# A PEER block's second down pass splits its stored activations again, with 9 of 32 blocks kept on chip

## The chip, the cores and the metric

The kernel runs on one core of one Trainium2 chip. A core has TensorE (matrix products; PE in the profile, and PEld for its weight loads), VectorE (DVE), ScalarE (ACT), GpSimd (POOL) and SyncE (SP), each with an instruction queue of its own that is executed in order. Data comes from HBM and goes back to it over 16 DMA engines. Here SP issues nearly all loads, POOL issues the indirect gathers and some stores, and ACT issues a few stores. The metric is the device time of one execution in microseconds.

## The reference, cut to what matters

```python
# D_MODEL 2048, 256 tokens, 8 PEER heads, 128 x 128 experts, 16 experts taken per head
mod = silu(c) @ w_ada + b_ada                     # 96 columns of 128 values: "ada"
h = rms_norm(x, g_norm1) * (1 + sc1) + sh1
x = x + gt1 * token_mixer(h, ...)                 # sparse attention, pooling, gates
h = rms_norm(x, g_norm2) * (1 + sc2) + sh2
# PEER: experts and gates from two product-key top-16 lists per head, then per token
a   = gelu(h . peer_u[experts])                   # up
out = sum_e (a * gate)[e] * peer_v[experts[e]]    # down
x = x + gt2 * out
```

All data is float32.

## The kernel before

**Token mixing.** The first part of the program does the ada sums, the input projection, the attention, the pooling branch and the output projection. Its order is made by a scheduler. Float32 weights arrive in tiles `raw` of 1 MB (128 x 2048), of which there are four in a ring (`RAW`). Each half of a tile is split into a rounded high part `wH` (ACT, line 124) and a rest `wL` (DVE, line 125), and TensorE multiplies the parts. An "ada" is one of the 96 columns of `mod`: a 1 MB load into the same ring, then a DVE multiply-and-sum over 128 x 2048 (line 139). 64 of them are not needed at once. They stand in a list `bg`, and the loops of the token mixing take from it at given rates: `R_Y` per round in the two loops of 16 rounds over `ybr` (the pooling branch, line 509, and the attention branch, line 532), `R_GA`, `R_WO` and `R_PQ` in others. The 16 last are GT2, needed only by the final step.

**PEER, done densely for 224 tokens.** From here on the order is written by hand: every engine runs its instructions in the order of the code. The *up* stage goes over all 128 x 128 experts, 128 at a time, in 256 halves `k`; a half is 16 matmuls against 1024 of the 2048 features, from a half tile of `u`. The activations of 128 experts go through Gelu and are stored to DRAM (`adram`). The gates are built as a dense table in DRAM (`gdram`) meanwhile. The *down* stage goes twice over 128 groups of 128 experts (`e`), 8 output blocks in each pass: pass 1 (`hf` 0) for features 0 to 1023, pass 2 (`hf` 1) for the rest. A group is again 16 matmuls, 8 of them 448 columns wide (high weights with both parts of the activations) and 8 of 224 (low weights with the high part). Weights are half tiles of `v`; one load brings two groups.

In pass 1 the activations of four groups are a block `h`, 32 blocks in all. For each block SP loads `ab` from `adram` (448 KB), for each two blocks a gate table `gb` from `gdram` (896 KB, one buffer); DVE multiplies (`gate_mul`, line 905), ACT and DVE split the product into the pair `aHL` (lines 910, 911), POOL stores the pair to `sdram` (896 KB, line 915), and in pass 2 SP loads it again (`gate_reload`, line 919; two buffers, freed by TensorE). Loads of `v` are issued three tiles ahead of use.

**PEER for the other 32 tokens** is done sparsely, beside all this: 32 gathers of 1 MB from the rows of `u` (one expert row for each of 128 token-and-slot partitions), each followed by a DVE multiply-and-sum (line 814), then 32 gathers from the rows of `v`, each followed by a DVE multiply-add (line 833). Two gather buffers: `fetch(n + 2)` is issued by POOL after the sum over buffer `n`. These, the routing, the gates and the leftover adas are one long generator of side work. After each half or group the code calls `spend(rate)`, which adds `rate` microseconds of DVE time to a credit and runs side work until it is used up:

```python
R_UP, R_D1, R_D2 = 0.85, 0.55, 0.9
def spend(budget):
    credit[0] = min(credit[0] + budget, 4.0)
    while credit[0] > 0.0:
        cost = next(work, "end")
        if cost is None or cost == "end":
            return cost
        credit[0] -= cost
```

So these rates set how fast gathers are asked for in the up stage, in pass 1 and in pass 2.

Of the kernel before, what the change touches and what calls it, by code (L numbers as in the profile page):

```python
# [9 lines left out]
F32 = mybir.dt.float32  # L10
F32R = mybir.dt.float32r
# [3 lines left out]
ALU = mybir.AluOpType  # L15
# [4 lines left out]
P = 128  # L20
T = 256
D = 2048
ND = 16
# [6 lines left out]
N = T - AS  # L30
# [1 line left out]
KGROUPS = ((0, 4), (4, 10), (10, 16))  # L32
NGU = 43
RAW = 4
R_K, R_Y, R_GA, R_WO, R_PQ = 0.6, 0.4, 0.7, 0.6, 0.3
TB = 8
R_UP, R_D1, R_D2 = 0.85, 0.55, 0.9
GATE_SCALE = 2.0 ** 15


# [1 line left out]
def kernel(  # L42
# [23 lines left out]
    nc = tc.nc  # L66
    wgrp_in = (wgrp0_in, wgrp1_in, wgrp2_in)
    dve, act, pe = nc.vector, nc.scalar, nc.tensor

    const = ctx.enter_context(tc.tile_pool(name="const", bufs=1))  # L70
    main = ctx.enter_context(tc.tile_pool(name="main", bufs=1))
    stream = ctx.enter_context(tc.tile_pool(name="stream", bufs=3))
    dram = ctx.enter_context(tc.tile_pool(name="dram", bufs=1, space=DRAM))
# [3 lines left out]
    hHL = main.tile([P, ND, 2, T], F32R, name="hHL")  # L77
# [211 lines left out]
    while ada_next[0]:  # L289
        f, i = ada_next[0].pop(0)  # L290
        f(i)
    for gi, (ka, kb) in enumerate(KGROUPS):
# [5 lines left out]
        for r in range(ntiles):  # L298
            us = list(range(per * r, min(per * r + per, NGU)))
            n = len(us) * nb * P  # L300
# [202 lines left out]
    for j in range(ND):  # L503
# [3 lines left out]
        for k in range(8):  # L507
            o = 1024 * (j % 2) + P * k
# [114 lines left out]
    px = ctx.enter_context(tc.tile_pool(name="px", bufs=1))  # L623
# [106 lines left out]

    gdram = dram.tile([P, N // 16, P, 16], F32, name="gdram")
    adram = dram.tile([P, P, N], F32, name="adram")
    sdram = dram.tile([P, P // 4, 4, 2, N], F32, name="sdram")
    made = {}

    def gates_build(x):
# [154 lines left out]
    def half(k):  # L891
        return split(raws[k // 2][:, 1024 * (k % 2):1024 * (k % 2) + 1024])

    def gate_load(h):
        made["ab", h] = px.tile([P, 4, N], F32, name="ab", bufs=3)
        nc.sync.dma_start(out=made["ab", h], in_=adram[:, 4 * h:4 * h + 4])

    def gate_table(b):
        made["gb", b] = px.tile([P, N // 16, 8, 16], F32, name="gb")
        nc.sync.dma_start(out=made["gb", b], in_=gdram[:, :, 8 * b:8 * b + 8])  # L900

    def gate_mul(h):
        i = 4 * (h % 2)
        av = made["ab", h].rearrange("p i (g t) -> p i g t", t=16)
        dve.tensor_tensor(av, av, made["gb", h // 2][:, :, i:i + 4].rearrange("p g i t -> p i g t"), ALU.mult)

    def gate_split(h):
        src = made["ab", h]
        aHL = px.tile([P, 4, 2, N], F32R, name="aHL", bufs=2)
        act.copy(aHL[:, :, 0], src)  # L910
        dve.tensor_tensor(aHL[:, :, 1], src, aHL[:, :, 0], ALU.subtract)
        made["act", h] = aHL

    def gate_store(h):
        nc.gpsimd.dma_start(out=sdram[:, h], in_=made["act", h].bitcast(F32))

    def gate_reload(h):
        aHL = px.tile([P, 4, 2, N], F32R, name="aHL", bufs=2)
        nc.sync.dma_start(out=aHL.bitcast(F32), in_=sdram[:, h])
        made["act", P // 4 + h] = aHL  # L920

    def mm2(ps, w, off, xHL, start, stop):
        wH, wL = w[0][:, off:off + P], w[1][:, off:off + P]
        pe.matmul(ps[:, :2 * N].rearrange("p (a n) -> p a n", a=2), wH, xHL, start=start, stop=False)  # L924
        pe.matmul(ps[:, :N], wL, xHL[:, 0], start=False, stop=stop)  # L925
# [9 lines left out]
    def ahead(k):  # L935
        if k % 2 == 0:
            fetch_tables(k // 2 + 3)
        if k + 2 < 4 * P:
            ws[k + 2] = half(k + 2)
        due = pend[:]  # L940
        del pend[:]
        for f in due:
            f()

    def up_add(e, ps):
        if e % 4 == 0:
# [12 lines left out]
    for k in range(2 * P):  # L959
        e, f = k // 2, k % 2  # L960
        ahead(k)
        if f == 0:
            ps = accp.tile([P, 512], F32, name="acc")
        w = ws.pop(k)
        for d in range(8):
            mm2(ps, w, d * P, hHL[:, 8 * f + d, :, AS:], f == 0 and d == 0, f == 1 and d == 7)
        if f == 1:
            pend.append(lambda e=e, ps=ps: up_add(e, ps))
        spend(R_UP)
        if k == 2 * P - 24:  # L970
            assert made["gates"] == T // TB - 1
            gate_table(0)
            for h in range(3):
                gate_load(h)
        if k in (2 * P - 8, 2 * P - 7):
            gate_mul(k - 2 * P + 8)
        if k == 2 * P - 6:
            gate_table(1)
        if k == 2 * P - 5:
            gate_split(0)  # L980
        if k == 2 * P - 4:
            gate_load(3)
            gate_store(0)

    def flush(j, ps, last):
        x, gt = xT[:, j, AS:], mod[:, GT2 + j:GT2 + j + 1]
# [21 lines left out]
    for hf in range(2):  # L1008
        assert hf == 0 or made["gt2"]
        po = [accp.tile([P, 512], F32, name="acc") if q < 6 else gps.tile([P, 512], F32, name="gp") for q in range(8)]  # L1010

        def products(e, w, j):
            mm2(po[j], w, P * j, made["act", 32 * hf + e // 4][:, e % 4], e == 0, e == P - 1)

        for e in range(P):
            k = 2 * P + P * hf + e
            h = e // 4
            if e < P - 1:
                ahead(k)
            if e < P - 2:  # L1020
                w = ws.pop(k)
                for j in range(8):
                    products(e, w, j)
            elif e == P - 1:
                w = [ws.pop(k - 1), ws.pop(k)]
                for j in range(8):
                    for i in range(2):
                        products(P - 2 + i, w[i], j)
                    flush(8 * hf + j, po[j], hf)
                ahead(k)  # L1030
            if hf == 0:
                b = e // 8
                if e % 8 in (3, 4) and b + 1 < P // 8:
                    gate_mul(2 * b + e % 8 - 1)
                if e % 8 == 5 and b + 2 < P // 8:
                    gate_table(b + 2)
                if e % 4 == 1 and h + 1 < P // 4:
                    gate_split(h + 1)
                if e % 4 == 2 and h + 1 < P // 4:
                    gate_store(h + 1)  # L1040
                    if h + 4 < P // 4:
                        gate_load(h + 4)
                if e == P - 2:
                    gate_reload(0)
            elif e % 4 == 1 and h + 1 < P // 4:
                gate_reload(h + 1)
            done = spend(R_D2 if hf else R_D1)
            if hf and done == "end" and "sum" not in made:
                made["sum"] = True
                pend.append(lambda: sparse_sum(po))  # L1050
                pend.append(lambda: pend.append(lambda: sparse_out(po)))
# [80 lines left out]
```

## Time and profile before

| | |
|---|---|
| median of 3 runs | 2226.87 us (2224.63 to 2232.24) |
| profiled execution | 2226.57 us, of which the span of the profile is 2224.8 us |
| busy share of the span | PE 94%, PEld 89%, DVE 75%, ACT 45%, POOL 6% |
| DMA | 677.91 MB, mean 305 GB/s |
| mean granted clock of TensorE | 0.968 of full speed |

Matmuls overlap in their pipeline, so the busy share of PE is not a share of its peak. What a stage loses is read from how many matmuls it completes in a stretch of time, and from who waits for whom there.

### The profile page before, as it was taken

How to read it: one execution, taken by the hardware profiler on the slowest of the kernel's cores; microseconds unless marked ns; L12 is line 12 of the kernel's file. 1: busy time of each engine (PE TensorE's matmuls, PEld its weight loads, DVE VectorE, ACT ScalarE, POOL GpSimd, SP SyncE). 2: the span in 40 equal slices, each digit the busy share in tenths (PEclk: the TensorE clock that was granted, in tenths of full speed). 3: DMA queues.
4: the chain of work that ended last, by engine and by line, in shares of the span. 5: the costliest groups of instructions: out<-in, count | busy, mean ns of one | idle time of the engine just before them, and what ended most of it. 6: DMA issues, size and time to landing. Idle time of an engine off the chain costs nothing.

```text
span 2224.8 us, 35362 instructions
## 1 busy us (share of the span) xinstructions
PE 2100.6 (94%) x14192; PEld 1981.4 (89%) x14192; DVE 1675.9 (75%) x2392; ACT 1011.9 (45%) x1373; POOL 136.5 (6%) x129
## 2 busy tenths in 40 slices
PE   6999999999989999999999999888899989999999
PEld 4899987999989999999999999777888888889998
DVE  7898877769787787778887776666777667777755
ACT  3543442754444455555555555343444334333334
POOL 0000000000000000000000000011112111222200
PEclk7999999999999999999999999988999999999999
DMA  8888875678775566776667778899999999999985
GB/s 340 328 318 309 309 264 217 227 294 311 288 280 193 186 225 234 252 258 238 235 225 256 259 281 294 337 332 373 403 392 400 397 378 389 415 412 415 415 309 199
DMA packets 146997, 677.91 MB, mean 305 GB/s; under 512 B 11737, under 2 KB 42481, under 8 KB 98321
## 3 DMA queue, kind: packets, MB, share of 16 engines
q1 hardware_dynamic: 125986, 549.63, 67.6%
q0 software_dynamic: 16240, 111.36, 12.4%
q10 hardware_dynamic: 4608, 14.68, 1.7%
q8 instruction: 111, 1.82, 0.3%
q14 instruction: 52, 0.43, 0.0%
HBM read 614.76 MB, written 60.83 MB: 304 GB/s over the span
## 4 chain that ended last, share of the span: by engine, by line
PE 57%; DMA 17%; issue 16%; DVE 7%; ACT 2%; POOL 0%; SPq 0%; ACTq 0%; DVEq 0%; POOLq 0%
PE acc L924 18%; PE acc L925 9%; PE acc L136 7%; PE acc L134 7%; PE acc L135 7%; DMA raw<-in_v_dram 6%; DMA raw<-in_ada_dram 6%; DMA aHL<-sdram 4%; PE gp L924 3%; DVE wL L125 3%; PE acc L509 2%; DVE raw L139 2%; PE gp L925 1%; ACT wH L124 1%; DMA raw<-in_wgrp_dram 1%
## 5 line engine op out<-in xcount | busy, mean ns | idle before, releaser
L124 ACT CAST wH<-raw 128x1024 fp32r<-128x1024 f32 (+2 forms) x738 | 750.8, 1022 | 1032.5 <-PE gp L924 311.4
L125 DVE TENSOR_TENSOR wL<-raw,wH 128x1024 fp32r<-128x1024 f32 (+2 forms) x738 | 871.3, 1188 | 387.5 <-ACT wH L124 385.2
L924 PE MATMUL acc<-hHL,wH 128*128 128x448 f32 x2048 | 653.4, 376 | 0.5 <-ACT r L600 0.5
L924 PE MATMUL acc<-aHL,wH 128*128 128x448 f32 x1536 | 526.2, 390 | 31.0 <-DMA aHL<-sdram 15.3
L925 PE MATMUL acc<-hHL,wL 128*128 128x224 f32 x2048 | 545.0, 266 | 10.9 <-DVE wL L125 10.8
L925 PE MATMUL acc<-aHL,wL 128*128 128x224 f32 x1536 | 421.8, 275 | 38.0 <-DVE wL L125 38.0
L924 PEld LDWEIGHTS acc<-hHL,wH 128*128 128x128 f32 x2048 | 385.3, 188 | 29.5 <-ACT r L600 0.7
L925 PEld LDWEIGHTS acc<-hHL,wL 128*128 128x128 f32 x2048 | 391.7, 191 | 12.3 <-DVE wL L125 12.3
L134 PE MATMUL acc<-hHL,wH 128*128 128x256 f32 x1200 | 344.9, 288 | 18.4 <-ACT wH L124 17.3
L924 PEld LDWEIGHTS acc<-aHL,wH 128*128 128x128 f32 x1536 | 302.5, 197 | 60.0 <-ACT wH L124 16.9
L925 PEld LDWEIGHTS acc<-aHL,wL 128*128 128x128 f32 x1536 | 307.8, 200 | 44.8 <-DVE wL L125 44.7
L136 PE MATMUL acc<-hHL,wL 128*128 128x256 f32 x1200 | 340.7, 286 | 5.3 <-DVE wL L125 5.2
L135 PE MATMUL acc<-hHL,wH 128*128 128x256 f32 x1200 | 341.6, 285 | 0.1
L139 DVE CUSTOM_DVE_ANT_0 raw<-raw,cb 128x2048 f32<-128x2048 f32 x96 | 219.6, 2287 | 67.2 <-DMA raw<-in_ada_dram 67.1
L134 PEld LDWEIGHTS acc<-hHL,wH 128*128 128x128 f32 x1200 | 232.0, 194 | 22.9 <-ACT wH L124 20.6
L136 PEld LDWEIGHTS acc<-hHL,wL 128*128 128x128 f32 x1200 | 231.2, 193 | 7.4 <-DVE wL L125 7.2
L135 PEld LDWEIGHTS acc<-hHL,wH 128*128 128x128 f32 x1200 | 232.4, 194 | 0.7 <-DVE hHL L573 0.3
L924 PE MATMUL gp<-aHL,wH 128*128 128x448 f32 x512 | 182.5, 386 | 0.0
L925 PE MATMUL gp<-aHL,wL 128*128 128x224 f32 x512 | 138.1, 270 | 0.0
L924 PEld LDWEIGHTS gp<-aHL,wH 128*128 128x128 f32 x512 | 100.1, 196 | 8.2
L925 PEld LDWEIGHTS gp<-aHL,wL 128*128 128x128 f32 x512 | 101.6, 198 | 0.0
L833 DVE SCALAR_TENSOR_TENSOR hs<-r,wS,hs 128x2048 f32<-128x2048 f32 x31 | 72.8, 2349 | 7.8 <-DMA r<-in_v_dram,idxS 7.8
(247 smaller groups left out, 1978.9 us busy)
## 6 DMA issues: line engine op xcount, KB each, us to landing
raw<-in_u_dram SPq DMA_DIRECT2D x128, 1024.0 KB, 5.1
raw<-in_v_dram SPq DMA_DIRECT2D x128, 1024.0 KB, 13.5
raw<-in_ada_dram SPq DMA_DIRECT2D x96, 1024.0 KB, 5.5
raw<-in_wgrp_dram SPq DMA_DIRECT2D x43, 768.0 KB, 6.1
sdram<-aHL POOLq DMA_DIRECT2D x32, 896.0 KB, 10.5
aHL<-sdram SPq DMA_DIRECT2D x32, 896.0 KB, 9.6
raw<-in_ybr_dram SPq DMA_DIRECT2D x16, 1024.0 KB, 5.4
raw<-in_wga_dram SPq DMA_DIRECT2D x16, 1024.0 KB, 4.8
```

Source lines behind the costliest of these rows:

```text
L124: act.copy(wH[:, :n], src)
L125: dve.tensor_tensor(wL[:, :n], src, wH[:, :n], ALU.subtract)
L134: pe.matmul(ps, wH, xH, start=start, stop=False, **kw)
L135: pe.matmul(ps, wH, xL, start=False, stop=False, **kw)
L136: pe.matmul(ps, wL, xH, start=False, stop=stop, **kw)
L139: dve.tensor_tensor_reduce(raw, raw, cb, scale=1.0, scalar=0.0, op0=ALU.mult, op1=ALU.add, accum_out=modr[:, i:i + 1])
L509: pe.matmul(ps, ybr[0][:, o:o + P], pooled[k], start=k == 0, stop=k == 7)
L833: dve.scalar_tensor_tensor(made["o"], rows, wS[:, n:n + 1], made["o"], op0=ALU.mult, op1=ALU.add)
L924: pe.matmul(ps[:, :2 * N].rearrange("p (a n) -> p a n", a=2), wH, xHL, start=start, stop=False)
L925: pe.matmul(ps[:, :N], wL, xHL[:, 0], start=False, stop=stop)
```

## The change

Pass 2 no longer loads split pairs. The gated product is written back as one float32 block (448 KB) over its place in `adram`, loaded again in pass 2 and split there again by ACT and DVE, so `gate_load` and `gate_split` now run over 64 block numbers. Nine of the 32 blocks (`h` = 3, 6, ... 27) are not stored at all: their product is written into the 32 KB per partition of `hHL`, which the up stage has finished with, and both passes split it from there. The rates change too: more adas in the two `ybr` loops (`R_Y`), more side work per half in the up stage (`R_UP`), less per group in the down passes.

```diff
-R_K, R_Y, R_GA, R_WO, R_PQ = 0.6, 0.4, 0.7, 0.6, 0.3
+R_K, R_Y, R_GA, R_WO, R_PQ = 0.6, 0.75, 0.7, 0.6, 0.3
-R_UP, R_D1, R_D2 = 0.85, 0.55, 0.9
+R_UP, R_D1, R_D2 = 0.97, 0.3, 0.75
+KEPT = 9
...
+    def kept(h):
+        return h % 3 == 0 and 0 < h <= 3 * KEPT
+
+    def gate_load(n):
+        h = n % (P // 4)
+        if n >= P // 4 and kept(h):
+            return
+        made["ab", n] = px.tile([P, 4, N], F32, name="ab", bufs=3)
+        nc.sync.dma_start(out=made["ab", n], in_=adram[:, 4 * h:4 * h + 4])
...
     def gate_mul(h):
+        if kept(h):
+            if "keep" not in made:
+                made["keep"] = main.tile([P, ND, 2, T], F32R, name="hHL").rearrange("p a b t -> p (a b t)")
+            o = 4 * N * (h // 3 - 1)
+            dst = made["keep"][:, o:o + 4 * N].bitcast(F32).rearrange("p (i n) -> p i n", n=N)
+            made["ab", P // 4 + h] = dst
+        else:
+            dst = made["ab", h]
...
+        made["ab", h] = dst
+        if not kept(h):
+            nc.gpsimd.dma_start(out=adram[:, 4 * h:4 * h + 4], in_=dst)
+
+    def gate_split(n):
+        src = made["ab", n]
...
-    def gate_store(h):
-        nc.gpsimd.dma_start(out=sdram[:, h], in_=made["act", h].bitcast(F32))
-
-    def gate_reload(h):
-        aHL = px.tile([P, 4, 2, N], F32R, name="aHL", bufs=2)
-        nc.sync.dma_start(out=aHL.bitcast(F32), in_=sdram[:, h])
-        made["act", P // 4 + h] = aHL
...
-                if e % 4 == 2 and h + 1 < P // 4:
-                    gate_store(h + 1)
-                    if h + 4 < P // 4:
-                        gate_load(h + 4)
-                if e == P - 2:
-                    gate_reload(0)
-            elif e % 4 == 1 and h + 1 < P // 4:
-                gate_reload(h + 1)
+            b, n = e // 8, 32 * hf + h
...
+            if e % 4 == 1 and n + 1 < 2 * (P // 4):
+                gate_split(n + 1)
+            if e % 4 == 2 and n + 4 < 2 * (P // 4):
+                gate_load(n + 4)
```

The change moves instructions on three queues. On POOL, at the end of the up stage and the start of pass 1, before (the `r_...` rows are gathers, `sdram<-aHL` the stores of pairs):

```order
L783 DMA gdram<-hs 128x2048 x14
L809 DMA r_14718<-in_urow_dram,idxS 128x2048 x7
L915 DMA sdram<-aHL 128x1792
L809 DMA r_14718<-in_urow_dram,idxS 128x2048
L915 DMA sdram<-aHL 128x1792
```

and at the same place in the changed program (its lines are numbered one higher):

```order
L783 DMA gdram<-hs 128x2048 x14
L809 DMA r_14327<-in_urow_dram,idxS 128x2048 x18
L923 DMA adram<-ab 128x896
L809 DMA r_14327<-in_urow_dram,idxS 128x2048
L923 DMA adram<-ab 128x896
```

18 gathers instead of 7 now stand ahead of the first store, and a store has half the bytes. Counted by the split of a weight half behind which they stand, before there are 6 `u` sums at halves 229 to 255 (with 6 adas among them), then 23 in pass 1 (with 6 adas) and 3 at the start of pass 2, and all 32 `v` sums in pass 2. In the changed program there are 19 `u` sums at halves 211 to 256 (with 2 adas), 13 `u` and 3 `v` sums in pass 1, and 29 `v` sums in pass 2, the last at its group 91 of 128.

On SP, in pass 2, before (`raw<-in_v_dram` are the weights, `aHL<-sdram` the pairs):

```order
L919 DMA aHL<-sdram 128x1792
L887 DMA raw<-in_v_dram 128x2x1024 x2
L919 DMA aHL<-sdram 128x1792
L887 DMA raw<-in_v_dram 128x2x1024 x2
L919 DMA aHL<-sdram 128x1792
```

and there in the changed program:

```order
L902 DMA ab<-adram 128x896
L887 DMA raw<-in_v_dram 128x2x1024 x2
L902 DMA ab<-adram 128x896
L887 DMA raw<-in_v_dram 128x2x1024 x4
L902 DMA ab<-adram 128x896
```

A pair of 896 KB for every two weight loads has become a block of 448 KB, and where a kept block falls there is no load. On DVE, in the middle of the attention branch of the token mixing, before (`ISA raw,modr` is an ada sum, `sg` and `m_...` the merging of the branches, `wL` a weight split):

```order
L139 ISA modr 128x1
L532 TENSOR_TENSOR sg<-acc,m_4880 128x256
L125 TENSOR_TENSOR wL<-raw,wH 128x1024
L533 TENSOR_TENSOR sg<-sg,r_253 128x256
L532 TENSOR_TENSOR sg<-acc,m_4944 128x256
L125 TENSOR_TENSOR wL<-raw,wH 128x1024
L536 TENSOR_TENSOR m_5684<-sg,pl 128x256
L533 TENSOR_TENSOR sg<-sg,r_253 128x256
L532 TENSOR_TENSOR sg<-acc,m_5005 128x256
L139 ISA raw,modr<-raw,cb 128x2048
```

and in the changed program:

```order
L533 TENSOR_TENSOR sg<-acc,m_4748 128x256
L140 ISA raw,modr<-raw,cb 128x2048
L140 ISA modr 128x1
L534 TENSOR_TENSOR sg<-sg,r_253 128x256
L533 TENSOR_TENSOR sg<-acc,m_4827 128x256
L140 ISA raw,modr<-raw,cb 128x2048
L140 ISA modr 128x1
L537 TENSOR_TENSOR m_5633<-sg,pl 128x256
L534 TENSOR_TENSOR sg<-sg,r_253 128x256
L533 TENSOR_TENSOR sg<-acc,m_4898 128x256
```

Between the first and the last row of line 532 (533 in the changed program) there are now 10 ada sums instead of 5 and 13 weight splits instead of 15. In the pooling branch (first to last row of line 510) there are 10 adas instead of 7, and the one ada that stood between the last output projection and the second normalisation is gone.

## Rows read from the trace of the kernel before

**Rows 1.** Windows by stage: start:end, length, each engine's busy time, PEclk, DMA share, GB/s.
```profile
318.00:405.00 87.00, 85.71 (x408) 66.43 (x408) 62.58 (x156) 23.83 (x61) 0.00 (x0) 0.98 0.53 197
511.00:560.00 49.00, 49.00 (x411) 49.00 (x410) 48.29 (x77) 23.13 (x33) 0.00 (x0) 1.00 0.89 320
...
768.00:1380.00 612.00, 611.31 (x4171) 578.59 (x4172) 480.71 (x796) 334.88 (x455) 16.82 (x26) 1.00 0.71 247
1380.00:1458.00 78.00, 67.57 (x411) 63.54 (x410) 53.38 (x56) 32.67 (x42) 7.29 (x6) 0.93 0.91 336
1458.00:1868.00 410.00, 355.76 (x2052) 329.80 (x2050) 288.68 (x267) 160.87 (x166) 56.19 (x56) 0.91 1.01 386
1868.00:2118.00 250.00, 237.72 (x1454) 224.37 (x1455) 187.52 (x136) 97.54 (x95) 53.02 (x32) 0.97 1.01 410
```
**Rows 2.** Timeline of DVE, end of pass 2: start, length, idle before and its releaser.
```profile
2135.03 1.23 DVE L125 TENSOR_TENSOR wL<-raw,wH 128x1024 fp32r<-128x1024 f32 x1 [1.28 <-ACT wH L124]
...
2212.74 1.22 DVE L125 TENSOR_TENSOR wL<-raw,wH 128x1024 fp32r<-128x1024 f32 x1 [1.28 <-ACT wH L124]
```
**Rows 3.** Timeline of TensorE's weight loads, between the two passes.
```profile
1868.47 0.29 PEld L924 LDWEIGHTS acc<-aHL,wH 128*128 128x128 f32 x1 [3.90 <-DVE xT L990]
```
**Rows 4.** Waits in pass 1: waiting engine, releaser, us in total, times, longest.
```profile
ACT wH L124 <- DMA raw<-in_v_dram: 128.7, 31, 9.5
...
PEld acc L925 <- DVE wL L125: 44.7, 23, 11.0
...
DVE raw L139 <- DMA raw<-in_ada_dram: 29.7, 6, 10.5
```
**Rows 5.** DMA in pass 1: the sum, then issues by tensor with KB each, us to landing.
```profile
DMA packets 56807, 158.10 MB, mean 386 GB/s; under 512 B 2777, under 2 KB 27904, under 8 KB 52924
...
raw<-in_v_dram SPq DMA_DIRECT2D x65, 1024.0 KB, 14.5
sdram<-aHL POOLq DMA_DIRECT2D x31, 896.0 KB, 10.3
ab<-adram SPq DMA_DIRECT2D x28, 448.0 KB, 12.2
gb<-gdram SPq DMA_DIRECT2D x14, 896.0 KB, 10.4
...
r<-in_urow_dram,idxS POOLq DMA_INDIRECT x25, 9.8
```
**Rows 6.** The same for pass 2 up to its last gather.
```profile
DMA packets 20181, 102.53 MB, mean 410 GB/s; under 512 B 1607, under 2 KB 1607, under 8 KB 15941
...
aHL<-sdram SPq DMA_DIRECT2D x22, 896.0 KB, 10.1
r<-in_v_dram,idxS POOLq DMA_INDIRECT x32, 10.0
```
**Rows 7.** Instructions by line, whole run: count | busy us, mean ns | idle before.
```profile
L139 DVE CUSTOM_DVE_ANT_0 raw<-raw,cb 128x2048 f32<-128x2048 f32 x96 | 219.6, 2287 | 67.2 <-DMA raw<-in_ada_dram 67.1
...
L814 DVE CUSTOM_DVE_ANT_0 r<-r,hs 128x2048 f32<-128x2048 f32 x32 | 73.1, 2285 | 0.0
...
L809 POOL DMA_INDIRECT r<-in_urow_dram,idxS x32 | 50.2, 1568 | 330.9 <-DVE aS L814 330.3 <-issue 0.6
...
L911 DVE TENSOR_TENSOR aHL<-ab,aHL 128x896 fp32r<-128x896 f32 x32 | 34.7, 1085 | 0.0
...
L910 ACT CAST aHL<-ab 128x896 fp32r<-128x896 f32 x32 | 30.0, 936 | 0.0
```
**Rows 8.** The chain that ended last, before the second normalisation.
```profile
656.07 2.20 DVE raw L139
```
**Rows 9.** Waits at the end of the up stage (1380 to 1458 us).
```profile
DVE raw L139 <- DMA raw<-in_ada_dram: 11.5, 2, 11.2
PEld acc L925 <- DVE wL L125: 11.3, 3, 9.8
```
**Rows 10.** Waits of SP's DMA queue in pass 1.
```profile
SPq L900 <- DVE ab L905: 121.6, 13, 14.1
```

More of the change, by code (lines that the diff above doesn't have):

```diff
@@ L732 @@
     adram = dram.tile([P, P, N], F32, name="adram")
-    sdram = dram.tile([P, P // 4, 4, 2, N], F32, name="sdram")
     made = {}
@@ L892, in half @@
         return split(raws[k // 2][:, 1024 * (k % 2):1024 * (k % 2) + 1024])
-    def gate_load(h):
-        made["ab", h] = px.tile([P, 4, N], F32, name="ab", bufs=3)
-        nc.sync.dma_start(out=made["ab", h], in_=adram[:, 4 * h:4 * h + 4])
+    def kept(h):
[6 more added lines that the diff above has]
+        nc.sync.dma_start(out=made["ab", n], in_=adram[:, 4 * h:4 * h + 4])
     def gate_table(b):
@@ L902, in gate_mul @@
     def gate_mul(h):
-        i = 4 * (h % 2)
[L904 to L908, printed above, removed]
+        if kept(h):
[6 more added lines that the diff above has]
+            dst = made["ab", h]
+        i = 4 * (h % 2)
+        dve.tensor_tensor(dst.rearrange("p i (g t) -> p i g t", t=16),
+                          made["ab", h].rearrange("p i (g t) -> p i g t", t=16),
+                          made["gb", h // 2][:, :, i:i + 4].rearrange("p g i t -> p i g t"), ALU.mult)
+        made["ab", h] = dst
[3 more added lines that the diff above has]
+        src = made["ab", n]
         aHL = px.tile([P, 4, 2, N], F32R, name="aHL", bufs=2)
@@ L911, in gate_split @@
         dve.tensor_tensor(aHL[:, :, 1], src, aHL[:, :, 0], ALU.subtract)
-        made["act", h] = aHL
-    def gate_store(h):
-        nc.gpsimd.dma_start(out=sdram[:, h], in_=made["act", h].bitcast(F32))
-    def gate_reload(h):
-        aHL = px.tile([P, 4, 2, N], F32R, name="aHL", bufs=2)
-        nc.sync.dma_start(out=aHL.bitcast(F32), in_=sdram[:, h])
-        made["act", P // 4 + h] = aHL
+        made["act", n] = aHL
     def mm2(ps, w, off, xHL, start, stop):
@@ L982 @@
             gate_load(3)
-            gate_store(0)
     def flush(j, ps, last):
@@ L1030 @@
                 ahead(k)
[L1031 to L1038, printed above, removed]
-                if e % 4 == 2 and h + 1 < P // 4:
-                    gate_store(h + 1)
-                    if h + 4 < P // 4:
-                        gate_load(h + 4)
-                if e == P - 2:
-                    gate_reload(0)
-            elif e % 4 == 1 and h + 1 < P // 4:
-                gate_reload(h + 1)
+            b, n = e // 8, 32 * hf + h
+            if hf == 0 and e % 8 in (3, 4) and b + 1 < P // 8:
+                gate_mul(2 * b + e % 8 - 1)
+            if hf == 0 and e % 8 == 5 and b + 2 < P // 8:
+                gate_table(b + 2)
+            if e % 4 == 1 and n + 1 < 2 * (P // 4):
+                gate_split(n + 1)
+            if e % 4 == 2 and n + 4 < 2 * (P // 4):
+                gate_load(n + 4)
             done = spend(R_D2 if hf else R_D1)
```

## The prediction

> **What bounds the kernel now.** I read the windows by stage first, to find where TensorE loses time; then the timeline of a stretch that loses none, for the floor; then the waits and the transfers of the stages that do.
>
> In the last 31 groups of pass 2 there is no gather and no wait but the regular one. DVE's weight splits start at 2135.03 and at 2212.74 us [rows 2], 77.71 us for 31 halves, so a half (16 matmuls) takes 2.507 us when nothing is late. A pass of 128 groups has a floor of 321 us.
>
> Pass 1 begins at 1458 and pass 2 at 1868.5 us [rows 3], so pass 1 takes 410 us: 89 us over its floor, 4 of them the wait of [rows 3], where TensorE needs accumulators that DVE is still emptying. Pass 2 has its last split at 2212.74 [rows 2], some two and a half groups before its end, which is then at about 2219: 350 us, 30 over. The end of the up stage, 1380 to 1458, completes 411 matmuls [rows 1], 411/16 x 2.507 = 64.4 us of work in 78: 13.6 lost. From 768 to 1380 TensorE is busy throughout.
>
> The reason in the passes is transfers. In pass 1 the DMA share is 1.01 and in pass 2, while gathers run, also 1.01, at 386 and 410 GB/s [rows 1]; TensorE waits for `wL`, and ACT ahead of it waits 128.7 us for `v` [rows 4]. What pass 1 asks for at its floor is 158 MB [rows 5] in 321 us, 492 GB/s. At the end of the up stage the DMA share is only 0.91; there the long wait is DVE's for an ada (11.2 us), and it holds up the split behind it for 9.8 us [rows 9]. An ada also keeps one of four ring places from `u` and `v`.
>
> **Pass 1: -65 us.** Bytes, with 1024 KB as 1.049 MB, from the counts in [rows 5]: the 31 stores of 896 KB become 21 of 448 KB (two more fall before the pass, nine blocks are kept): 28.4 to 9.6 MB. The 25 gathers become 16: 26.2 to 16.8. Six adas go: -6.3. Two reloads of pairs become three loads of single blocks, 31 loads in all: 14.2. The 65 loads of `v`, 68.2 MB, and 14 of `gb`, 12.9 MB, stay. Sum 121.7 MB, which in 321 us is 379 GB/s. That is under the 410 that the queues hold when they only read, and about the 386 of the old pass 1, whose figure contains its ada stalls. So the floor is in reach on average, but with at most 8% to spare. What remains is burst: SP waits for the single `gb` buffer 121.6 us in 13 times [rows 10], 9.4 us each, with the `v` loads queued behind it, and this order is unchanged. Below, nothing is lost (then 321 + 4); above, I let each of the 16 gate tables cost 3 us, about a third of such a wait, 48 us. I take 20, nearer the lower end, because a `v` load is asked for three tiles, some 15 us, ahead, and its landing, now 14.5 us, must fall with the load. 321 + 4 + 20 = 345 instead of 410.
>
> A new wait lies here: a buffer of `ab` is now free only when its store has landed, and SP waits for that in front of `v` loads. In the order of the program most such loads come six or seven groups (15 us) behind their product, five come three groups behind (7.5 us). A store of twice the size lands in 10.3 us [rows 5]. I put that inside the 20.
>
> **Pass 2: -23 us.** To the last gather at its group 91 it takes 228 us at the floor, and needs 46 `v` loads (48.2 MB), 15 single blocks (6.9) and 27 gathers (28.3): 83.4 MB, 366 GB/s against the 410 that it holds [rows 6]. The wait for reloaded pairs goes with them. In their place come 32 splits on ACT of 0.936 us and on DVE of 1.085 us [rows 7]. Per group DVE then has one weight split (1.22, rows 2), 1.085/4 and side work of 0.75: 2.24 of 2.507 us; before it was 1.22 + 0.9. The cover is 0.27 us a group; without it the new splits would cost 32 x 1.085 = 35 us. I leave a loss of 7 (the floor of it 3, for the start of the pass; above, 20): 30 to 7.
>
> **End of the up stage: -1 us.** From half 209 to 256, 47 halves or 118 us at the floor, the transfers are 23.5 of `u` and `v` (24.7 MB), 20 gathers (21.0), 2 adas (2.1), 2 `gb` and 4 `ab` (3.7) and the stores of activations (3.7): 55 MB, 467 GB/s. At 410 they take 134 us, 16 over the floor; three tiles loaded ahead can lend some of it. I take 13 lost in place of the 13.6 by adas. Bounds: 0, if the lead lends it all, and 46, at the 336 GB/s of this stretch now [rows 1]. DVE has 1.22 + 0.97 = 2.19 of 2.507 us here before the sums of the stage's own results, so a late gather is hardly made up.
>
> **Token mixing: +9 us.** An ada sum is 2.287 us [rows 7]. In the attention branch (511 to 560) DVE is busy 48.29 of 49 us while TensorE is busy all 49 [rows 1]: both are full. Five more sums there are 11.4 us of DVE work without cover. The output projection behind it needs the last merged block within its first output, so little can be put off. I take +10 (0 to 15). The pooling branch has 87 - 62.6 = 24 us of idle DVE [rows 1] for three more sums, 6.9 us; that is cover for them, and I take +1 (0 to 7 without it). The ada before the second normalisation, 2.20 us on the chain [rows 8], is gone: -2.
>
> **Sum.** -65 - 23 - 1 + 9 = -80. The profiled execution took 2226.57 us (span 2224.8 and 1.8 around it), 0.3 from the median of 2226.87. Forecast 2147 us.
>
> **The rivals.**
> *Everything hidden.* The loads ahead even the bursts out: pass 1 loses 8 with its 4, pass 2 4, the up stage nothing. 2147 - 16 - 3 - 13 = 2115. For it: 379 and 366 GB/s are both below what was held. Against: the stretches of [rows 1] in which TensorE is busy throughout run at 247 and 320 GB/s; none shows 379 without waits.
> *The gate tables set the pace of pass 1.* Each costs 3 us as bounded above: 48 instead of 20, 2175. For it: the wait in [rows 10] has the same order of loads. Against: DVE reaches the product sooner with less side work.
> *The rate is not held.* With more small blocks and writes among reads the queues keep only 336 GB/s, the least of the full stretches in [rows 1]. Up stage 55/336 = 164 us (+46 over the floor), pass 1 121.7/336 = 362 + 4, pass 2 83.4/336 = 248 and 93 more + 4: 2226.6 + 9 + 32 - 44 - 5 = 2218. Against: the 386 of pass 1 was kept with 28 MB of stores in it, and 410 for 250 us in pass 2 [rows 1]. The Trainium skill (HBM Reference, "Specifications") has such a limit: about 358 GB/s per core, half of a stack's rate, though it adds that a core streaming alone measures well above its share. By its figure the three stretches take 154, 340 and 233 us and the sum is some 2172; the 410 of [rows 1], on the only core that runs, speaks against it.
> *Slower: late gathers in the up stage.* A sum over a gather comes two periods after its request; at R_UP a period is 2.37/0.97 x 2.507 = 6.1 us, so 12.2 us, for 1.6 us of issue [rows 7] and 9.8 of landing [rows 5]. It is tight, and DVE waits in order, with the weight splits behind. If 467 GB/s of demand stretches landing to L, a period is (L + 1.6)/2. With 20 gathers the 93 us gained elsewhere are lost at a period of 10.8, L = 20 us; at L = 22 the loss is 20 x 5.7 = 114 and the time 2248. Against: `v` loads in pass 1, at full queues, land in 14.5 [rows 5].
>
> **How the numbers follow.** Forecast 0.60, all hidden 0.15, gate tables 0.15, rate not held 0.05, late gathers 0.05. The range 2113 to 2182 takes in the first three with their bounds and leaves out the last two, about 0.1, and as much for terms that miss together. 0.3%, about 6.7 us, is what a measurement can tell from no change. Faster 0.92 (the first three and half of the rate case, whose 2218 lies near that limit), same 0.03, slower 0.05.
>
> **What would show it.** Right: pass 1 near 345 and pass 2 near 328 us between the first matmuls with `aHL`; DMA share below 1 in both; no wait of TensorE for reloads; the stretch between the first and last merged block about 10 us longer; ACT's wait for `v` down from 128.7 us to some 30. Wrong: a wait of about 3 us in every eighth group of pass 1, DVE waiting for gathers by more than 10 us in the up stage, or SP waiting long for stores in front of `v` loads.

## The result and the profile after

The changed kernel takes 2161.62 us (median of 4 runs, 2156.86 to 2165.35); beside it the kernel before took 2229.55 (4 runs, 2224.63 to 2238.09, one more than in the table ahead of the prediction). The ratio is 0.969, 95% interval 0.965 to 0.973: faster by some 68 us. The profiled execution of the changed kernel took 2165.35 us, 61.2 less than that of before (2226.57), and the comparison by stage below is between these two.

The windows by stage show where they went (columns as in [rows 1]; code lines after the new constant have moved by one, and by nine or ten near the end):

```profile
338.00:411.00 73.00, 71.37 (x326) 55.84 (x327) 58.89 (x140) 15.06 (x34) 0.00 (x0) 0.95 0.71 261
...
524.00:589.00 65.00, 55.27 (x396) 53.98 (x395) 60.54 (x89) 22.66 (x33) 0.00 (x0) 0.87 0.89 317
...
794.00:1400.00 606.00, 602.74 (x4110) 569.91 (x4109) 488.33 (x801) 329.46 (x447) 25.04 (x31) 1.00 0.72 255
1400.00:1486.00 86.00, 79.76 (x474) 74.58 (x473) 70.45 (x74) 38.08 (x49) 20.61 (x14) 0.94 0.98 375
1486.00:1822.00 336.00, 325.27 (x2029) 305.50 (x2028) 247.06 (x223) 161.06 (x164) 46.96 (x38) 0.99 1.00 366
1822.00:2060.00 238.00, 236.76 (x1506) 225.41 (x1505) 205.78 (x163) 120.69 (x124) 46.44 (x27) 1.00 0.96 367
```

Pass 1 is the fifth row: 336 us for what took 406 by the same bounds (410 in [rows 1], whose window goes on to the first matmul of pass 2). The up stage begins at 794 instead of 768. The second row is the attention branch with the step to the output projection: 65 us, where [rows 1] has 49 for the same work (396 and 411 matmuls recorded), and the granted clock in it is 0.87, where it was 1.00.

The waits of pass 1 (engine, releaser, us in total, times, longest) answer to [rows 4]:

```profile
ACT wH L125 <- DMA raw<-in_v_dram: 64.2, 23, 5.5
...
PEld acc L935 <- DVE wL L126: 11.0, 19, 1.1
```

TensorE's waits for `wL` fell from 44.7 to 11.0 us, and none is longer than 1.1. ACT still waits for `v`, but half as long. What SP's queue waits for there answers to [rows 10] (L906 loads a gate table, L902 a block of `ab`):

```profile
SPq L906 <- DVE ab L918: 93.7, 9, 11.4
SPq L906 <- DVE hHL L918: 48.5, 5, 10.8
...
SPq L902 <- DMA adram<-ab: 24.6, 8, 11.6
```

The first two together are the old wait for the single gate-table buffer, 142 us in 14 times. The third is the new wait for a store, in front of `v` loads; it is there, eight times, and TensorE's waits above show that the loads ahead absorb it.

The transfers of pass 1 answer to [rows 5] (sum; then issues with count, KB each, us to landing):

```profile
DMA packets 51534, 123.04 MB, mean 366 GB/s; under 512 B 2389, under 2 KB 27477, under 8 KB 49207
...
raw<-in_v_dram SPq DMA_DIRECT2D x64, 1024.0 KB, 11.4
ab<-adram SPq DMA_DIRECT2D x31, 448.0 KB, 9.6
...
adram<-ab POOLq DMA_DIRECT2D x21, 448.0 KB, 7.1
...
r<-in_urow_dram,idxS POOLq DMA_INDIRECT x12, 7.8
r<-in_v_dram,idxS POOLq DMA_INDIRECT x5, 8.8
```

The bytes are 123.0 MB instead of 158.1, and every landing is shorter (`v` 11.4 against 14.5 us).

### The profile page after: what moved, and what is told of

Same layout as the page of the kernel before. It is cut to its first block, busy times and chain, and to the rows that moved or that the text cites. A ratio compares the mean times of both kernels' runs of the same rounds, so it can differ in the third digit from the quotient of the medians.

```text
span 2163.6 us, 35340 instructions
## 1 busy us (share of the span) xinstructions
PE 2080.1 (96%) x14192; PEld 1965.9 (91%) x14192; DVE 1704.4 (79%) x2424; ACT 1039.6 (48%) x1405; POOL 142.5 (7%) x120
## 3 DMA queue, kind: packets, MB, share of 16 engines
q0 software_dynamic: 13472, 92.55, 11.4%
## 4 chain that ended last, share of the span: by engine, by line
PE 47%; issue 24%; DMA 13%; DVE 10%; ACT 3%; POOL 1%; SPq 0%; DVEq 0%; ACTq 0%; POOLq 0%
PE acc L934 16%; PE acc L935 8%; DMA raw<-in_ada_dram 6%; PE acc L137 5%; DMA raw<-in_v_dram 5%; PE acc L135 5%; PE acc L136 5%; PE gp L934 4%; DVE raw L140 4%; DVE wL L126 3%; PE gp L935 2%; ACT wH L125 2%; DMA raw<-in_u_dram 1%; PE acc L510 1%; DMA r<-in_urow_dram,idxS 0%
## 5 line engine op out<-in xcount | busy, mean ns | idle before, releaser
L934 PE MATMUL acc<-aHL,wH 128*128 128x448 f32 x1536 | 503.6, 378 | 7.6 <-DVE ast L961 5.0
L935 PE MATMUL acc<-aHL,wL 128*128 128x224 f32 x1536 | 409.6, 267 | 6.5 <-DVE wL L126 6.2
L934 PEld LDWEIGHTS acc<-aHL,wH 128*128 128x128 f32 x1536 | 290.8, 189 | 29.8 <-DVE ast L961 5.3
L935 PEld LDWEIGHTS acc<-aHL,wL 128*128 128x128 f32 x1536 | 296.2, 193 | 12.2 <-DVE wL L126 12.1
L137 PEld LDWEIGHTS acc<-hHL,wL 128*128 128x128 f32 x1200 | 231.5, 194 | 11.8 <-DVE wL L126 11.5
L934 PE MATMUL gp<-aHL,wH 128*128 128x448 f32 x512 | 177.1, 377 | 0.4 <-DVE xT L998 0.4
L814 DVE CUSTOM_DVE_ANT_0 r<-r,hs 128x2048 f32<-128x2048 f32 x32 | 73.2, 2287 | 15.1 <-DMA r<-in_urow_dram,idxS 15.1
```

Source lines behind the costliest of these rows:

```text
L137: pe.matmul(ps, wL, xH, start=False, stop=stop, **kw)
L814: dve.tensor_tensor_reduce(rows, rows, made["h"], scale=1.0, scalar=0.0, op0=ALU.mult, op1=ALU.add, accum_out=aS[:, n:n + 1])
```

## The experiments

Twelve more kernels ran. All times in this table are from their profiled executions, except the last column. *Pooling and gate* runs from the first pooled output to the first merged block of the attention branch; *attention* from there to the first output of the output projection; *up* from the first matmul of the up stage to the first with `aHL`; *pass 1* from there to the first sum into `xT`, and *pass 2* from that to the same sum of pass 2.

| kernel | pooling and gate | attention | up begins at | up | pass 1 | pass 2 | median us |
|---|---|---|---|---|---|---|---|
| before | 178.1 | 49.7 | 767.9 | 690.4 | 405.9 | 351.2 | 2229.55 |
| changed | 185.4 | 64.6 | 793.6 | 692.3 | 336.7 | 331.6 | 2161.62 |
| 1: `R_Y` back | 176.3 | 49.3 | 762.6 | 701.7 | 340.1 | 330.0 | 2148.11 |
| 2: sums later | 182.1 | 50.5 | 771.3 | 692.5 | 336.9 | 328.9 | 2141.08 |
| 3: none kept | 184.8 | 62.2 | 787.6 | 690.9 | 346.9 | 330.1 | 2169.85 |
| 4: rates alone | 184.1 | 62.7 | 788.4 | 689.5 | 361.7 | 340.1 | 2191.44 |
| 5: five searches | 178.2 | 49.8 | 773.3 | 700.3 | 337.9 | 330.5 | 2152.25 |
| 6: five loads | 177.8 | 57.9 | 775.5 | 696.9 | 341.3 | 333.2 | 2157.81 |
| 7: attention back | 182.9 | 49.4 | 771.7 | 696.8 | 340.6 | 331.5 | 2150.44 |
| 8: pooling back | 177.0 | 58.5 | 773.7 | 699.1 | 337.0 | 333.6 | 2158.57 |
| 9: five sums | 181.9 | 60.8 | 784.2 | 696.7 | 341.5 | 333.3 | 2167.93 |
| 10: five places | 181.2 | 49.2 | 771.6 | 698.9 | 340.0 | 331.7 | 2155.80 |
| 11: queries at 1.0 | 176.3 | 49.4 | 765.4 | 696.2 | 330.7 | 331.7 | 2138.85 |
| 12: less in the mix | 178.9 | 50.7 | 770.8 | 690.3 | 335.5 | 331.7 | 2142.39 |

**1. The sums of the token mixing undone.**

```diff
-R_K, R_Y, R_GA, R_WO, R_PQ = 0.6, 0.75, 0.7, 0.6, 0.3
+R_K, R_Y, R_GA, R_WO, R_PQ = 0.6, 0.4, 0.7, 0.6, 0.3
```

> The changed kernel with R_Y back at 0.4, so that both branch loops of the token mixing hold as many ada sums as before; ten more ada rows then fall behind the PEER queries, eight ahead of the first down product and two in pass 1. Theory (DVE work without cover in the branch loops): the up stage starts 18 to 26 us earlier, at 768 to 776 us, and the ten rows push 10.5 MB of ada and displaced gathers into the passes, at some 375 GB/s up to 28 us; total 2150 to 2170, about the changed kernel's 2162. Rival 1 (the 26 us lost before the up stage are not the sums' but a slower execution): the up stage starts at 790 or later again, total 2175 to 2190. Rival 2 (an ada row in the up stage costs nothing, its 2.3 us lie in idle time of DVE and its bytes in idle time of the queues): 2136 to 2144.

The up stage begins at 762.6, 31 us earlier, and the ten rows cost 9.4 us in the up stage and 3.4 in pass 1. Total 2148.11: this part of the change loses 13.5 us by the medians. Both rivals fall, and the theory was right in its direction only: both numbers lie below its ranges. The later price was less than my 28 us: eight of the ten rows fell in the up stage, whose first 606 us have a DMA share of only 0.72 (windows above), and cost 1.2 us each there.

**2. The same sums, but later.**

```diff
-R_K, R_Y, R_GA, R_WO, R_PQ = 0.6, 0.75, 0.7, 0.6, 0.3
+R_K, R_Y, R_GA, R_WO, R_PQ = 0.6, 0.4, 0.7, 0.9, 0.65
```

> R_Y back at 0.4, R_WO 0.9 and R_PQ 0.65: the sums leave the branch loops and go to the output projection and the PEER queries, where DVE was idle for 22 and some 23 us in the kernel before; four rows instead of two are left for the up stage. Theory: four or five more sums in each stage are 9 to 11 us of DVE work under 22 us of idle time, so they cost 0 to 6 us together; the up stage starts at 768 to 776, the rest keeps 692 + 341 + 331 us and the total is 2136 to 2148. Rival 1 (the loss is not in the branch loops but comes with any earlier ada row, since each takes one of four ring places from the weights): the up stage starts at 785 to 794, total 2155 to 2165. Rival 2 (a slower execution): as rival 1, without longer waits for weights in the two stages.

2141.08 us, in the theory's range. From the first output to the up stage it took 203.8 us with eight more sums in it, against 205.6 before: there they are free.

**3. No block kept on chip.**

```diff
-KEPT = 9
+KEPT = 0
```

> The changed kernel with KEPT = 0: all 32 blocks of gated activations are stored and loaded again, nothing else changes. Theory (the passes are set by their bytes): nine more stores of 448 KB, 4.1 MB in pass 1 at some 375 GB/s, are 11 us; nine more loads, 4.1 MB mostly in pass 2, whose queues are busy for 0.95 to 0.98, are another 0 to 11: total 2170 to 2184, pass 1 at 348 to 354. Rival (the bursts round the gate tables set pass 1, not the sum of bytes, and the kept blocks only fill idle queues): pass 1 stays at 339 to 343 and the total within 2158 to 2166.

Pass 1 grew by 10.2 us, as the bytes said (129.1 MB), and pass 2 not at all: the nine loads cost nothing there. Pass 1 (346.9) and the total, 2169.85, lie just below the theory's ranges; the rival falls.

**4. The kernel before with the five new rates.**

```diff
-R_K, R_Y, R_GA, R_WO, R_PQ = 0.6, 0.4, 0.7, 0.6, 0.3
+R_K, R_Y, R_GA, R_WO, R_PQ = 0.6, 0.75, 0.7, 0.6, 0.3
-R_UP, R_D1, R_D2 = 0.85, 0.55, 0.9
+R_UP, R_D1, R_D2 = 0.97, 0.3, 0.75
```

> The kernel before with only the five numbers of the change (R_Y 0.75, R_UP 0.97, R_D1 0.3, R_D2 0.75): the split pairs of 896 KB are still stored and loaded. Theory (bytes set the passes): token mixing loses the same 22 to 26 us, pass 1 sheds six ada rows and nine gathers, 15.7 of 158.1 MB, so 369 us at 386 GB/s instead of 410, pass 2 sheds up to 3 gathers, 8 us: total 2193 to 2215. Rival 1 (the gain of the change comes from the moved gathers and sums alone): 2158 to 2175. Rival 2 (the stores of pairs alone set pass 1, what else is moved is hidden): pass 1 at 400 or more, total 2235 to 2255.

2191.44, a little under the theory's range: pass 1 361.7 and pass 2 340.1. Both rivals fall. The rates alone give 44 us of the 69 in pass 1 and 11 of the 20 in pass 2. The transfers of its pass 1, the sum and the issues of `v` and of the stores:

```profile
DMA packets 54302, 142.28 MB, mean 394 GB/s; under 512 B 2515, under 2 KB 27603, under 8 KB 52041
...
raw<-in_v_dram SPq DMA_DIRECT2D x64, 1024.0 KB, 14.4
sdram<-aHL POOLq DMA_DIRECT2D x31, 896.0 KB, 9.0
```

So pass 1 went in three steps: 156.4 MB in 405.9 us, 142.3 in 361.7 (rates), 129.1 in 346.9 (single blocks instead of pairs, kernel 3), 123.0 in 336.7 (nine kept). The first 14 MB went with 3.1 us each, the next 13 with 1.1 and the last 6 with 1.7, so a byte has no one price here.

The first step took more away than bytes, since the six adas of pass 1 went with it. In the kernel before, DVE waits for their loads in front of its weight splits, and TensorE waits behind it. The first of them, on DVE and on TensorE:

```profile
1463.76 2.29 DVE L139 CUSTOM_DVE_ANT_0 raw<-raw,cb 128x2048 f32<-128x2048 f32 x1 [10.47 <-DMA raw<-in_ada_dram]
```

```profile
1469.47 0.56 PE L925 MATMUL acc<-aHL,wL 128*128 128x224 f32 x1 [10.69 <-DVE wL L125]
```

Five of the six longest gaps of TensorE in that pass (10.7, 5.1, 4.9, 4.7 and 2.9 us) stand behind such a wait. The windows of pass 1, before and in kernel 4:

```profile
1458.00:1864.00 406.00, 354.92 (x2048) 329.25 (x2047) 284.85 (x256) 159.08 (x162) 55.21 (x55) 0.91 1.01 385
```

```profile
1478.00:1839.00 361.00, 334.10 (x2029) 308.71 (x2028) 247.34 (x222) 157.63 (x163) 46.55 (x48) 0.98 1.02 394
```

TensorE's idle time fell from 51.1 to 26.9 us. The other 21 us of the gain are busy time for the same products, at a granted clock of 0.91 and then of 0.98. How much of the 44 us fewer gathers alone would have given, with the adas left in, was not tried.

**5. DVE work alone in the attention branch, first try.**

```diff
         pace(R_Y)
+        if j % 3 == 2:
+            dve.max(out=idle8, in_=cb)
```

> The kernel of the first experiment (R_Y 0.4) with five maximum searches over 2048 columns of a constant row added to the attention branch on DVE, in every third of its 16 merged blocks, and no load: some 2.2 us each if they run like the ada sums. The results go nowhere. The stretch from the first merged block to the first output of the output projection was 49.3 us in the first experiment and 64.6 in the changed kernel. Theory (DVE has no room there): it is 60 to 65 us again, 11 us of DVE work and 0 to 4 of lower granted clock behind it, total 2158 to 2164. Rival (the five ada loads cost, by ring places and bytes, and the sums fit): 49 to 52 us, total 2146 to 2152.

This tested nothing. The searches depend on no data of the branch, and in the trace all five ran between 10.5 and 79.8 us, at the start of the program. The attention stretch was 49.8 us without them.

**6. Loads alone.**

```diff
         pace(R_Y)
+        if j % 3 == 2:
+            dve.tensor_copy(idle8[:, 0:1], load(ada_in[j])[:, 0:1])
```

> The kernel of the first experiment with five loads of an ada row added to the attention branch, at the same places, of which DVE copies only one column: 1 MB and a ring place each, hardly any DVE time. Theory: the stretch stays within 49 to 53 us, total 2146 to 2152. Rival (ring places and bytes): 56 to 65 us, total 2155 to 2164.

The stretch is 57.9 us: the theory fell and the rival was right. Five loads with hardly any DVE work behind them cost 8.6 us. The window of the stretch and the two waits that show it:

```profile
512.00:570.00 58.00, 51.98 (x411) 50.93 (x411) 50.96 (x82) 23.26 (x33) 0.00 (x0) 0.97 0.93 344
```

```profile
ACT wH L125 <- DMA raw<-in_ybr_dram: 6.3, 2, 4.3
...
PEld acc L135 <- ACT wH L125: 4.0, 3, 2.8
```

TensorE is busy 51.98 of 58 us; ACT waits for a row of `ybr` up to 4.3 us, and TensorE for ACT's half of it.

**7. The old rate in the attention branch only.**

```diff
         dve.tensor_tensor(mL[j], sg, mH[j], ALU.subtract)
-        pace(R_Y)
+        pace(0.4)
```

> The changed kernel with the old rate 0.4 in the attention-branch loop alone; the pooling loop keeps 0.75. Five or six sums fewer in the attention branch; they go mostly to the up stage, as in the first experiment. Theory: the stretch from the first merged block to the first output falls from 64.6 to 49 to 52 us, the wait ahead of it (pooling and its gate, some 5 us) stays: up stage starts at 770 to 778; half of the price that the first experiment paid later (9 us in the up stage, 3 in pass 1), some 6: total 2147 to 2156. Rival (the pooling loop makes the debt that the attention branch pays): the stretch stays above 56 us, total 2156 to 2164.

49.4 us in the attention stretch, 182.9 in pooling and gate: as the theory had it.

**8. The old rate in the pooling loop only** (the same edit at the end of the pooling loop).

> The changed kernel with the old rate 0.4 in the pooling loop alone; the attention branch keeps 0.75. Theory: the stretch from the first merged block to the first output stays at 61 to 65 us, pooling and its gate get 3 to 7 us shorter, some 6 us are paid later: total 2158 to 2167, about as the changed kernel. Rival (debt from the pooling loop): the stretch falls below 56 us, total 2146 to 2154.

58.5 us, between the two: the price of the attention branch is mostly its own, but the stretch is 4 to 6 us shorter when the pooling loop holds fewer sums. Nine sums stand between its first and last merged block here, ten in the changed kernel, so some 2 of these us are one sum's work. Pooling and gate are back at 177.0. The window of the stretch:

```profile
512.00:570.50 58.50, 52.34 (x398) 50.77 (x396) 56.66 (x87) 22.46 (x32) 0.00 (x0) 0.94 0.91 333
```

Against kernel 1, with five sums, it is 9.2 us longer for four more sums and their loads, and four sums are 9.1 us of DVE work.

**9. Sums alone.**

```diff
-            ybr[0] = load_split(ybr_in[b, j // 2])
+            raw = load(ybr_in[b, j // 2])
+            ybr[0] = [split(raw[:, 1024 * i:1024 * i + 1024]) for i in range(2)]
+            if j in (2, 4, 8, 10, 14):
+                dve.tensor_tensor_reduce(raw, raw, cb, scale=1.0, scalar=0.0, op0=ALU.mult, op1=ALU.add,
+                                         accum_out=idle1)
```

> The kernel of the first experiment with five sums of the ada kind (multiply and sum over 2048 columns) added to the attention branch over rows of ybr that lie there already, right behind their splits: DVE work of 5 x 2.29 = 11.4 us, no load. The results go nowhere. The stretch from the first merged block to the first output of the output projection: 49.3 us in the first experiment, 57.9 with five loads alone, 62 to 65 with both. Theory now (two prices that meet): 53 to 59 us, total 2152 to 2158. Rival 1 (DVE has no room, and the loads of the sixth experiment hid the same 11 us in another way): 60 to 65 us, total 2158 to 2164. Rival 2 (the loads alone): 49 to 52 us, total 2146 to 2151.

60.8 us: rival 1, and with it the prediction's own account. 11.4 us of DVE work cost 11.5. The window and the waits:

```profile
517.00:578.00 61.00, 52.04 (x412) 50.97 (x411) 60.28 (x88) 23.66 (x34) 0.00 (x0) 0.97 0.71 251
```

```profile
PEld acc L137 <- DVE wL L126: 8.9, 4, 3.6
```

DVE is busy 60.28 of 61 us at a DMA share of 0.71, and TensorE waits for it four times. The whole kernel took 2167.93, above that rival's total and more than these 11.5 us over the first experiment's; its pooling and gate were also longer (181.9 against 176.3), ahead of the edit. Kernels 1, 2, 9, 10 and 11 run the same instructions in the same order up to the last pooled output, and yet their pooling loops took from 67.9 to 73.8 us, so much do executions differ there.

**10. Ring places alone.**

```diff
+            raw = stream.tile([P, D], F32, name="raw", bufs=RAW)
+            nc.sync.dma_start(out=raw[:, :P], in_=ada_in[j][:, :P])
+            dve.tensor_copy(idle8[:, 0:1], raw[:, 0:1])
```

> As the sixth experiment, but each of the five added loads brings 128 of 2048 columns, 64 KB instead of 1 MB: the same ring places at the same points, hardly any bytes. Theory (bytes: the DMA share there was 0.97 to 0.98 in the sixth experiment): 49 to 52 us in the stretch, total 2146 to 2152. Rival (places: the weights behind come later because four places are all there are): 55 to 58 us, total 2154 to 2160.

49.2 us. The same places at the same points cost nothing when they bring 64 KB; what costs in the sixth experiment is the 5.2 MB. The median, 2155.80, is above the theory's total, but not by the stretch: in the profiled execution the first pooled output came 3.5 us later than in kernel 1 and pooling and gate took 4.9 longer, ahead of the edit.

**11 and 12. Two more divisions of the sums.**

```diff
+R_K, R_Y, R_GA, R_WO, R_PQ = 0.6, 0.4, 0.7, 0.9, 1.0
...
+R_K, R_Y, R_GA, R_WO, R_PQ = 0.6, 0.2, 0.7, 1.0, 0.9
```

> The kernel of the second experiment (R_Y 0.4, R_WO 0.9) with R_PQ at 1.0 in place of 0.65: all sums are done before the up stage. Theory: the four rows that leave the up stage gave 1.2 us each there by the first experiment (ten rows against two, 9 us), and DVE has room in the PEER queries: 2134 to 2141. Rival (the queries' stage becomes full, as the attention branch was): the stretch from the first output to the up stage, 203.8 us, grows by 4 to 9: 2141 to 2150.

> R_Y 0.2, R_WO 1.0, R_PQ 0.9: six more sums leave the two branch loops, below the number that the kernel before had there; three are left for the up stage. Theory (every sum and load there has a price, 1.3 us in the pooling loop and 2.5 in the attention branch): 3 to 9 us less than the second experiment, 2132 to 2139, if the output projection takes its one or two more in idle time. Rival 1 (at 0.4 the branch loops were already free of loss, TensorE busy for all of them): 2138 to 2144. Rival 2 (the later stages become full): 2144 to 2155.

The eleventh kernel is the best of all: 2138.85 us (5 runs), ratio to before 0.961 (0.959 to 0.963), and so some 23 us faster than the changed kernel. It is the changed kernel with no more sums in the branch loops than before and all of them done before the up stage; the reason given for it does not hold, though, since its up stage took 696.2 us against 692.5 of the second, and its lead of 2 us over the second is within their spread (2135.5 to 2141.0 and 2137.8 to 2147.5). The twelfth took 2142.39: rival 1. Below the old number of sums in the two loops nothing was gained; its attention stretch was 50.7 us. The windows of the eleventh, attention and then output projection to the up stage:

```profile
510.00:560.00 50.00, 50.00 (x420) 50.00 (x419) 49.72 (x79) 23.78 (x34) 0.00 (x0) 1.00 0.90 324
560.00:765.00 205.00, 196.96 (x1581) 193.22 (x1580) 176.64 (x304) 87.24 (x129) 0.00 (x0) 0.98 0.83 302
```

In the second row DVE is busy 176.64 of 205 us, and the stretch is no longer than the 205.6 us of before.

## Why the prediction was right, and where a term was off

The forecast was 2147 us; the median came to 2161.62 and the profiled execution to 2165.35.

**Pass 1** was forecast to lose 65 us and lost 69 (405.9 to 336.7). By these bounds, which end ahead of the wait between the passes, it is 16 us over the floor of 321, where the forecast had 20 for bursts. The mechanism named, fewer bytes against that floor, is shown for the last 25 us of the gain (kernel 4 to kernel 3 to the changed kernel); the other 44 came with the rates, and in them are also the waits of DVE for adas and a lower clock of TensorE (kernel 4). The forecast counted up from the floor, so it did not depend on telling these apart. The gate tables do not set the pace: TensorE's longest wait for `wL` is 1.1 us, where that rival needs some 3 in each. The mark "a DMA share below 1" was wrong: it is 1.00 in the window above, at 366 GB/s, and the stage is nevertheless within 5% of its floor. ACT's wait for `v` came down to 64.2, not to some 30; it costs little, since ACT runs ahead.

**Pass 2** was forecast at -23 and came to -20 (351.2 to 331.6). No wait for reloaded data is left in it, and its DMA share is 0.96. The new splits are covered: DVE is busy 205.78 of 238 us, TensorE 236.76. The step of counting by bytes came within 3 us, but of the 20 us the rates alone gave 11 (kernel 4), and the kept blocks none (kernel 3).

**The end of the up stage** was forecast at -1 and the whole stage came to +2 (690.4 to 692.3). From 1400 to 1486, 474 matmuls are 474/16 x 2.507 = 74.3 us of work, so 11.7 are lost, where I took 13. DVE does wait for late gathers, and TensorE behind it, in small pieces:

```profile
DVE r L814 <- DMA r<-in_urow_dram,idxS: 11.6, 6, 3.6
ACT wH L125 <- DMA raw<-in_u_dram: 7.6, 2, 5.4
PEld acc L935 <- DVE wL L126: 7.4, 4, 3.5
```

```profile
1457.28 2.29 DVE L814 CUSTOM_DVE_ANT_0 r<-r,hs 128x2048 f32<-128x2048 f32 x1 [3.63 <-DMA r<-in_urow_dram,idxS]
```

```profile
1460.77 0.56 PE L935 MATMUL acc<-hHL,wL 128*128 128x224 f32 x1 [3.22 <-DVE wL L126]
```

The first sum is just over the 10 us that I had set as a mark for the slower rival. Each of TensorE's three gaps there (2.0, 0.8 and 3.2 us) follows such a wait, so the late gathers are there and cost some 6 us of idle TensorE, far from the loss that rival needs.

**The rate** was held: 366 and 367 GB/s in the passes, where less was asked, 394 over the 361 us of pass 1 in kernel 4. The Trainium skill (HBM Reference, "Specifications (TRN2)") gives about 358 GB/s as a core's share, and adds that a core streaming alone measures well above it, about 425; the runs agree with the addition, and the 358 bounds nothing here.

**The token mixing** is the term that was mis-sized: +9 in the forecast, +25.7 between the two profiled executions, 31 against kernel 1. With it alone at its measured size the sum -80 becomes -63, beside the profiled -61.2; that the rest agrees so well is in part luck, since the other three terms were off by -4, +3 and +3 us and nearly cancel. Its parts:

- *The attention branch*, +10 in the forecast, is +13.4: 62.2 to 64.6 us in the three kernels with the rate of the change in both loops (mean 63.2), 49.3 to 50.7 in the seven with the old rate or less and nothing added that ran in the branch (mean 49.8). The DVE account carries most of it: 11.4 us of work cost 11.5 (kernel 9), where the forecast took 10. The loads alone cost 8.6 us by their bytes (kernel 6), since a ring place costs nothing (kernel 10), but the two prices overlap: 11.5 and 8.6 alone, 13.4 together. The windows of the stretch in kernels 3 and 4:

```profile
520.40:582.60 62.20, 54.33 (x417) 53.08 (x417) 60.15 (x88) 24.47 (x34) 0.00 (x0) 0.95 0.92 324
```

```profile
520.90:583.60 62.70, 54.16 (x400) 52.44 (x399) 60.16 (x89) 22.61 (x33) 0.00 (x0) 0.92 0.90 326
```

DVE is busy for some 60 us in all four kernels with five more sums. Its idle time in the stretch is under 1 us without added loads (kernel 9) and 2 to 4.5 us with them, and that is what the forecast left out. With four more sums and their loads but the old rate in the pooling loop, nothing came on top of the sums (kernel 8); whether the rest is the loads' own or comes with the pooling loop stays open.

- In the profiled execution of the change a third thing is in it. Ten-microsecond windows from the second third of the branch on:

```profile
534.00:544.00 10.00, 9.37 (x79) 9.17 (x77) 10.00 (x16) 4.04 (x7) 0.00 (x0) 1.00 0.95 327
544.00:554.00 10.00, 7.71 (x49) 7.30 (x49) 9.15 (x15) 3.96 (x6) 0.00 (x0) 0.83 0.91 329
554.00:564.00 10.00, 7.14 (x56) 6.88 (x55) 9.88 (x16) 2.87 (x5) 0.00 (x0) 0.91 0.96 346
564.00:574.00 10.00, 10.00 (x67) 10.00 (x67) 8.10 (x12) 3.10 (x6) 0.00 (x0) 0.75 0.73 282
574.00:584.00 10.00, 6.78 (x44) 6.58 (x44) 10.00 (x15) 3.73 (x6) 0.00 (x0) 0.77 0.88 319
```

TensorE idles for 2 to 3 of 10 us in three of them, and from the second on its granted clock is below 1.00; in the fourth it is busy throughout and yet completes 67 matmuls, where a full ten microseconds hold 84 (411 in 49 us). A clock of 0.75 in such a window means half of it at 1.2 and half at 2.4 GHz. Over the 65 us of the stretch TensorE is idle 9.7 and busy 55.3; at the granted 0.87 that is 48 us of work at the full clock, so by this estimate some 7 us are clock. With sums or loads alone the clock was 0.97, and the same estimate gives 1.6. These microseconds do not add to the price of DVE's work, since DVE is idle for only some 4.5 of the 65. Kernels 3 and 4 run the same instructions there, at 0.95 and 0.92, and take 62.2 and 62.7 us where this one takes 64.6: the execution with the lowest clock was the longest, by some 2 us, but that the clock made it so is not shown.

- *Pooling and its gate*, +1 in the forecast, is +5.5: 182.9 to 185.4 us in the four kernels with the new rate in the pooling loop (mean 184.3), 176.3 to 182.1 in the other ten (mean 178.8). The rows of the pooled outputs and of the merged blocks, before and then changed, part it at the last pooled output:

```profile
L510 DVE TENSOR_TENSOR r<-acc,r x16: 404/419/426, 334.5 to 404.8; 128x256 f32<-128x256 f32 x16
L532 DVE TENSOR_TENSOR sg<-acc,m x16: 416/420/425, 512.6 to 556.2; 128x256 f32<-128x256 f32 x16
```

```profile
L511 DVE TENSOR_TENSOR r<-acc,r x16: 349/420/428, 338.8 to 410.6; 128x256 f32<-128x256 f32 x16
L533 DVE TENSOR_TENSOR sg<-acc,m x16: 419/423/429, 524.2 to 579.0; 128x256 f32<-128x256 f32 x16
```

The pooling loop itself took 71.5 to 73.4 us with the new rate and 67.7 to 73.8 with the old (means 72.0 and 70.1), so the forecast's +1 for it stands within the spread. From there to the first merged block it is 111.4 to 113.6 against 107.8 to 110.0 (means 112.3 and 108.6): some 4 us in the gate, for which the forecast had nothing. The gate holds 11 or 12 sums in the former and 10 to 12 in the latter, so it is not the price of more sums there; its cause stays open.

- *The step before the second normalisation*, -2 in the forecast, is -1 at most (205.6 to 204.8 us from the first output to the up stage).
- The rest, some 8 us of the 25.7, lies ahead of the first pooled output (338.8 against 334.5 us) and in the spread of single executions: the up stage begins between 787.6 and 793.6 in three kernels that do not differ ahead of it. Two more ada sums stand ahead of the first pooled output in these (48 instead of 46), but it came anywhere from 331.5 to 338.8 us with the old rate, so I do not explain it by the change.

## What to carry to other kernels

A stage in which both the engine that feeds TensorE and TensorE itself are full has no room for background work, and its price there has two sides, which overlap: the instruction on the feeding engine and the bytes of its load, each of which has to be looked up in that stage alone. Before moving work out of a transfer-bound stage, list the idle time of every other stage: here the same ten sums cost some 19 us in two loops, 13 in the up stage and pass 1 (kernel 1), and eight of them nothing in the output projection and the PEER queries (kernel 2), a choice worth 23 us in the end. An added instruction that is to load a stage must depend on that stage's data; check in the trace that it ran there.

## What the runs showed of the hardware

The busy share of the DMA engines says little about how near a limit is. It was 1.01 at 386 GB/s in pass 1 of before, 1.02 at 394 in kernel 4, and 1.00 at 366 in the changed kernel, where less was asked and every landing was shorter (`v` 14.5, 14.4 and 11.4 us). The landing time told the relaxed pass from the other two; the share did not.
